# A planner that lets only one of ACT and DVE read a PSUM bank at a time

## The chip, the cores and the metric

One core of one Trainium2 chip runs the kernel. The metric is the device time of one execution in microseconds; 576.35 us is the median of three runs before the change (576.04 to 577.06).

## The reference

The kernel computes a trunk of two decoder layers on one sequence of 256 tokens, with 1024 features, in float32. Layer 0 mixes tokens by causal attention with 16 heads of 64 (with 256 tokens there is a single block of keys, so the choice of past blocks selects nothing). Layer 1 mixes them by attention with 12 heads in three groups, windows and dilations (128, 1), (512, 4) and (2048, 16), whose results are weighted by their softmax denominators. After each mixer stands a squared-ReLU MLP of width 4096. Cut to what matters:

```python
cos, sin = rotary_tables(S, x.dtype)
for i in range(2):
    mix = (moba_attention, dilated_attention)[i](h, w_qkv[i], w_o[i], cos, sin)
    h = layer_norm(ALPHA * h + mix, ln_mix_g[i], ln_mix_b[i])
    h = layer_norm(ALPHA * h + jnp.square(jax.nn.relu(h @ w_in[i])) @ w_out[i], ln_mlp_g[i], ln_mlp_b[i])

# in both mixers, before the scores
q = apply_rotary(qkv[:, :, 0], cos, sin) * (dh ** -0.5)
k = apply_rotary(qkv[:, :, 1], cos, sin)
# apply_rotary: [t1 * c - t2 * s, t2 * c + t1 * s]
```

## The kernel before

**The arithmetic.** Every float32 operand of a matmul is split in two parts of a narrower type, a high part (ACT copies it, line 316) and a low part (DVE subtracts, line 321), and each product is made of three matmuls: high by high, high by low, low by high. The weights arrive as tiles of 128x1024 (`raw`, four buffers, loads on SP, line 312) and become `whi` and `wlo`, ten buffers each. Matmuls are recorded on line 325, transposes on line 615.

**The banks.** PSUM has eight banks, tiles of 128x512 float32, under two tags of four each. `acc` holds the projections and the output sums; `tp` holds scores, transposes and the attention results.

**Attention.** A pair of heads goes through these steps: two weight tiles are projected into one `acc` bank (q in its left half, k in its right); `rotate` (line 530) turns that bank into the split, rotated q and k; the score matmuls fill `tp` banks; DVE adds the mask and takes the minimum (line 591); ACT takes the exponential (line 601); DVE scales (line 608); PE transposes into a `tp` bank; ACT copies that to `pt` (line 623); PE multiplies by v; and the result is split into `ahi` and `alo`. Layer 0 has 8 such pairs, layer 1 has 6. Two softmax-free stages follow in each layer: the output projection with its LayerNorm, and the MLP, whose weights make up most of the kernel's bytes.

**The rotation.** ACT copies the bank's lower 64 partitions to the upper half of a tile b and the upper to the lower (two instructions, line 544). DVE multiplies the bank by the first table into tile a (line 520), multiplies b by the second table in place, and adds b to a. Then ACT makes the high parts of q (line 316) and k (line 556), and DVE the low parts (lines 321 and 559, the latter through the helper of line 527). So three instructions read the bank: two of ACT and one of DVE. The copies and the multiply have no data in common but the bank.

**What sets the order.** Instructions aren't written in the order in which they run. Each is recorded as an operation with an engine, a cost in us and the buffers that it reads and writes. `Plan.order` (line 138) makes a first pass without contention for due times, and then simulates: for each engine it takes the operations that could start first (`start_of`, line 170: when the operands are there, the engine is free and a buffer of the tag is free), among these the one with the earliest due time, and of all engines the one that starts earliest; where two start at the same time ACT comes ahead of DVE. DVE may pass over a ready operation for a more urgent one that is about to be ready, if that saves over 0.2 us (`PATIENT`). Loads keep the order in which they were recorded. Costs are formulas, a copy of a half bank 512/1200 + 0.055 + 0.1 us, the multiply 512/960 + 0.07, and a result of ACT is there for DVE, or of DVE for ACT, after `LAT` = 0.14 us. The result is one list, sorted by simulated start, and it is emitted in that order; each engine then works through its share in order. The semaphores are set by the layer below, from the emitted order.

The dependences that the planner knows come from the buffers' readers and writers: a read after a write, a write after a read or a write. Two reads of one buffer are independent.

Of the kernel before, what the change touches and what calls it, by code (L numbers as in the profile page):

```python
# [54 lines left out]
def latency(p, q):  # L55
    if p.eng == "SP":
        return LANDED
    if p.eng == "PE":
        return 0.0 if q.eng == "PE" else PE_OUT
    return PE_IN if q.eng == "PE" else LATS.get((p.eng, q.eng), LAT)  # L60
# [3 lines left out]
def landed(t, bus, nbytes):  # L64
    t = max(t + FETCH, bus)
    return t + nbytes / RATES[t > BURST]


class Buf:


    def __init__(self, pool, shape, dtype, tag, name):
        self.pool, self.shape, self.dtype, self.tag, self.name = pool, shape, dtype, tag, name
        self.real = None
        self.state = {}
        self.left = 0
        self.held = False

    @property
    def t(self):  # L80
# [9 lines left out]
class Plan:  # L90
# [47 lines left out]
    def order(self):  # L138
        clock = {e: BEGIN[e] for e in ("PE", "SP")}
        bus = 0.0  # L140
        for o in self.ops:
            t = max([clock.get(o.eng, 0.0)] + [p.end + latency(p, o) for p in o.preds])
            o.end = t + o.cost
            if o.eng in clock:
                clock[o.eng] = o.end
            if o.xfer:
                bus = o.end = landed(t, bus, o.xfer)
            o.due = t - o.ahead if o.eng == "PE" else None
        t = clock["PE"]
        for o in reversed(self.ops):  # L150
            for q in o.succs:
                d = q.due - o.cost - latency(o, q)
                o.due = d if o.due is None else min(o.due, d)
            if o.due is None:
                o.due = t - o.early
        engines = sorted({o.eng for o in self.ops})
        free = {e: BEGIN[e] for e in engines}
        bus = 0.0
        cand = {e: [] for e in engines}
        slots = {tag: [0.0] * cap for tag, cap in self.caps.items()}  # L160
        done = []
        for o in self.ops:
            o.wait = len(o.preds)
            o.ready = 0.0
            if not o.wait:
                cand[o.eng].append(o)

        loads = [o for o in self.ops if o.eng == "SP"]

        def start_of(o):  # L170
            s = max(o.ready, free[o.eng])
            need = {}
            for b in o.bufs:
                if not b.held:
                    need.setdefault(b.tag, []).append(b)
            for tag, bs in need.items():
                q = self.queue[tag]
                spare = 0
                if {id(b) for b in q[: len(bs)]} != {id(b) for b in bs}:
                    if tag not in LOOSE:  # L180
                        return None
                    spare = 1
                if len(slots[tag]) < len(bs) + spare:
                    return None
                s = max(s, sorted(slots[tag])[len(bs) - 1])
            return s

        total = len(self.ops)
        while len(done) < total:
            best = None  # L190
            for e in engines:
                lst = [(start_of(o), o) for o in cand[e] if e != "SP" or o is loads[0]]
                lst = [x for x in lst if x[0] is not None]
                if not lst:
                    continue
                first = min(s for s, _ in lst)
                s, o = min((x for x in lst if x[0] <= first), key=lambda x: (x[1].due, x[1].n))
                if e in PATIENT:
                    worst = PATIENT[e]
                    now, ready = s, o  # L200
                    for s2, o2 in lst:
                        if now < s2 < now + ready.cost and o2.due < ready.due:
                            waits = max(s2 - o2.due, s2 + o2.cost - ready.due)
                            runs = max(now - ready.due, now + ready.cost - o2.due)
                            if runs - waits > worst:
                                worst, s, o = runs - waits, s2, o2
                if best is None or s < best[0]:
                    best = (s, o)
            assert best is not None
            s, o = best  # L210
            cand[o.eng].remove(o)
            if o.eng == "SP":
                loads.pop(0)
            for b in o.bufs:
                if not b.held:
                    slots[b.tag].remove(min(slots[b.tag]))
                    self.queue[b.tag].remove(b)
                    b.held = True
            cost = o.cost * 2 if o.eng == "PE" and s < PE_COLD else o.cost
            free[o.eng] = s + cost  # L220
            o.end = s + cost
            if o.xfer:
                bus = o.end = landed(s, bus, o.xfer)
            done.append((s, o.n, o))
            for b in o.bufs:
                b.left -= 1
                b.last = max(getattr(b, "last", 0.0), o.end + (PE_OUT if o.eng == "PE" else LAT))
                if not b.left:
                    slots[b.tag].append(b.last)
            for q in o.succs:  # L230
                q.wait -= 1
                q.ready = max(q.ready, o.end + latency(o, q))
                if not q.wait:
                    cand[q.eng].append(q)
        done.sort(key=lambda x: x[:2])
        return [o for _, _, o in done]
# [7 lines left out]


LOOSE = ("tp",)


LAYOUT = (
# [866 lines left out]
```

## Time and profile before

| what | value |
|---|---|
| median of three runs | 576.35 us |
| the profiled execution, its time | 576.27 us |
| the profiled execution, its span from the first to the last instruction | 574.5 us |
| mean granted TensorE clock | 0.997 |
| busy, PE (matmul) / PEld (weight load) | 561.4 / 486.1 us |
| busy, DVE / ACT / POOL | 418.9 / 313.8 / 8.4 us |
| instructions in the span | 8588 |
| moved by DMA | 105.61 MB, 184 GB/s on average |

Busy time of an engine is the time in which at least one of its instructions runs; weight loads overlap matmuls. In lists of instructions the first number is the start in us from the beginning of the span, the second the duration, then the engine, the line, the operation and the tiles (result<-operands); "x2" merges instructions that follow each other, and a bracket at the end gives how long the engine was idle before it and whose end it waited for. In lists of waits the columns are the total in us, the number of waits and the longest. Attention of layer 0 takes the span to about 110 us, its MLP lies between about 137 and 290, attention of layer 1 between about 312 and 375, and its MLP between about 403 and 566.

### The profile page before, as it was taken

What the parts mean: (1) busy time and instruction counts of PE and PEld (TensorE: products, weight loads), DVE (VectorE), ACT (ScalarE), POOL (GpSimd) and SP (SyncE); (2) the same over time, 40 slices, a digit from 0 to 9 for tenths busy, and PEclk for the clock granted to TensorE, in tenths of its full rate; (3) what the DMA queues carried; (4) which work ended last, traced back from release to release, by engine and by line L of the source; (5) the groups of instructions that cost most, each with busy time, mean ns of one, the idle gap of its engine ahead of it and who ended that gap; (6) DMA issues with size and microseconds to landing.
All of it is one profiled execution on the core that took longest, in us unless ns stands there. A gap on an engine that the chain in (4) does not pass through costs nothing.

```text
span 574.5 us, 8588 instructions
## 1 busy us (share of the span) xinstructions
PE 561.4 (98%) x3234; PEld 486.1 (85%) x3234; DVE 418.9 (73%) x729; ACT 313.8 (55%) x529; POOL 8.4 (1%) x13
## 2 busy tenths in 40 slices
PE   8999999999999999999999999999999999999994
PEld 7898898788888888888888997878888888888884
DVE  5898879798775675675678698878966756756644
ACT  6887878456554554455533586844754544544400
POOL 0000000010000000000000000000000000000000
PEclk9999999999999999999999999999999999999998
DMA  8676753627877565555526534534888655655101
GB/s 323 222 242 210 245 184 111 193 83 242 266 274 241 186 212 185 186 189 182 189 80 176 215 129 136 177 111 139 266 261 252 210 187 177 194 186 181 37 1 73
DMA packets 30282, 105.61 MB, mean 184 GB/s; under 512 B 3489, under 2 KB 4257, under 8 KB 30241
## 3 DMA queue, kind: packets, MB, share of 16 engines
q1 hardware_dynamic: 30240, 105.07, 55.8%
q8 instruction: 25, 0.41, 0.3%
q14 instruction: 17, 0.13, 0.1%
HBM read 104.01 MB, written 1.05 MB: 183 GB/s over the span
## 4 chain that ended last, share of the span: by engine, by line
PE 87%; DMA 4%; ACT 4%; DVE 3%; issue 1%; SPq 0%; DVEq 0%; ACTq 0%
PE acc L325 49%; PE tp L325 36%; DMA raw<-in_wv_dram 2%; PE tp L615 2%; ACT whi L316 1%; DVE wlo L321 1%; ACT ta L544 1%; DVE ta L520 1%; DMA raw<-in_wqk_dram 1%; DMA raw<-in_xw_dram 1%; ACT sc L601 0%; DVE tok L527 0%; DVE klo L527 0%; ACT pt L623 0%; ACT khi L556 0%
## 5 line engine op out<-in xcount | busy, mean ns | idle before, releaser
L321 DVE TENSOR_TENSOR wlo<-raw,whi 128x1024 fp32r<-128x1024 f32 (+2 forms) x185 | 222.0, 1206 | 91.4 <-ACT whi L316 91.0
L316 ACT ACTIVATE whi<-raw 128x1024 fp32r<-128x1024 f32 (+2 forms) x184 | 191.0, 1047 | 147.8 <-PE tp L325 69.9
L325 PE MATMUL acc<-whi,ahi 128*128 128x512 f32 (+1 forms) x312 | 119.5, 383 | 0.0
L325 PE MATMUL acc<-wlo,ahi 128*128 128x512 f32 (+1 forms) x312 | 117.3, 380 | 0.0
L325 PE MATMUL tp<-xs,whi 128*128 128x512 f32 x448 | 112.0, 392 | 0.0
L325 PE MATMUL acc<-whi,alo 128*128 128x512 f32 (+1 forms) x312 | 100.7, 379 | 0.0
L325 PEld LDWEIGHTS tp<-xs,whi 128*128 128x128 f32 x448 | 81.1, 189 | 14.9
L325 PEld LDWEIGHTS acc<-whi,ahi 128*128 128x128 f32 x312 | 58.7, 188 | 11.3 <-issue 0.9
L325 PEld LDWEIGHTS acc<-wlo,ahi 128*128 128x128 f32 x312 | 58.7, 188 | 10.4
L325 PE MATMUL acc<-xs,whi 128*128 128x256 f32 x448 | 65.1, 287 | 0.9 <-ACT xs L316 0.6
L325 PEld LDWEIGHTS acc<-whi,alo 128*128 128x128 f32 x312 | 57.1, 188 | 10.5
L325 PEld LDWEIGHTS tp<-xs,wlo 128*128 128x128 f32 x448 | 61.0, 190 | 4.2
L325 PE MATMUL tp<-xs,wlo 128*128 128x256 f32 x448 | 62.6, 283 | 0.0
L325 PEld LDWEIGHTS acc<-xs,whi 128*128 128x128 f32 x448 | 58.6, 192 | 3.0 <-ACT xs L316 1.1
L316 ACT ACTIVATE ahi<-ta 128x256 fp32r<-128x256 f32 x56 | 22.8, 407 | 27.6 <-DVE ta L527 27.5
L325 PE MATMUL acc<-xs,wlo 128*128 128x256 f32 x224 | 36.5, 284 | 0.0
L325 PEld LDWEIGHTS acc<-xs,wlo 128*128 128x128 f32 x224 | 31.0, 192 | 0.7 <-issue 0.7
L325 PE MATMUL acc<-whi,xs 128*128 128x512 f32 (+1 forms) x112 | 28.2, 362 | 0.0
L321 DVE TENSOR_TENSOR alo<-ta,ahi 128x256 fp32r<-128x256 f32 x56 | 23.4, 421 | 6.2 <-ACT ahi L316 6.2
L520 DVE TENSOR_TENSOR ta<-tp,ta 128x256 f32<-128x256 f32 x56 | 23.5, 420 | 5.8 <-ACT ta L769 5.8
L769 ACT ACTIVATE ta<-tp 128x256 f32<-128x256 f32 x56 | 21.0, 375 | 9.3 <-PE tp L325 9.3
L544 ACT ACTIVATE ta<-acc 64x512 f32<-64x512 f32 x28 | 16.6, 593 | 17.4 <-DVE ta L520 11.2
(85 smaller groups left out, 531.8 us busy)
## 6 DMA issues: line engine op xcount, KB each, us to landing
raw<-in_win_dram SPq DMA_DIRECT2D x64, 512.0 KB, 4.3
raw<-in_wout_dram SPq DMA_DIRECT2D x64, 512.0 KB, 4.2
raw<-in_wqk_dram SPq DMA_DIRECT2D x24, 512.0 KB, 4.3
raw<-in_wo_dram SPq DMA_DIRECT2D x14, 512.0 KB, 3.4
raw<-in_wv_dram SPq DMA_DIRECT2D x8, 512.0 KB, 6.7
g<-in_lng_dram SPq DMA_DIRECT2D x4, 512.0 KB, 5.8
b<-in_lnb_dram SPq DMA_DIRECT2D x4, 512.0 KB, 7.8
raw<-in_wv1a_dram SPq DMA_DIRECT2D x4, 512.0 KB, 3.3
```

What stands on the lines that cost most here:

```text
L316: op("ACT", act(n, sbuf=sbuf), lambda: nc.scalar.activation(hi(), src(), AF.Copy), r, whi)
L321: lambda: nc.vector.tensor_tensor(lo(), src(), f32(hi()), op=ALU.subtract), list(r) + list(whi), wlo,
L325: nc.tensor.matmul(out_ap, lhsT, rhs, start=start, stop=stop)
L520: op("DVE", dve(n) + extra, lambda: nc.vector.tensor_tensor(out_ap(), a(), b(), op=alu), r, w)
L544: lambda h=h: nc.scalar.activation(b.t[64 * h : 64 * h + 64, :], ps.t[64 - 64 * h : 128 - 64 * h, :], AF.Copy),
L615: nc.tensor.transpose(ps.t[:, c : c + P], src(), ident.t)
L769: op("ACT", act(S), lambda: nc.scalar.activation(u(), ps.t[:, S:], AF.Copy), [ps], uk)
```

## The change

Each buffer remembers the last operation outside PE that was placed on it. When the planner asks when an operation of ACT or DVE could start, and this operation uses a buffer of one of the PSUM tags whose last such operation was another engine's, the start is no earlier than that operation's end plus the latency between the two engines (0.14 us between ACT and DVE). The first pass, the due times, the costs and the instructions themselves stay as they are; only the order in which they are emitted can differ. The whole diff:

```diff
@@ class Buf
         self.left = 0
         self.held = False
+        self.reader = None
@@ Plan.order, start_of
             for b in o.bufs:
                 if not b.held:
                     need.setdefault(b.tag, []).append(b)
+                elif b.tag in BANKS and o.eng != "PE" and b.reader and b.reader.eng != o.eng:
+                    s = max(s, b.reader.end + latency(b.reader, o))
@@ Plan.order, after an operation is placed
             for b in o.bufs:
+                if o.eng != "PE":
+                    b.reader = o
                 b.left -= 1
@@
 LOOSE = ("tp",)
+
+BANKS = ("tp", "acc")
```

## The prediction

> **What bounds the kernel now.** I read the page first, then the busy times by stretch, then the waits, then the timelines of the engines around each wait. The page says who is full and which group carries the instructions that the change is about:
>
> ```profile
> PE 561.4 (98%) x3234; PEld 486.1 (85%) x3234; DVE 418.9 (73%) x729; ACT 313.8 (55%) x529; POOL 8.4 (1%) x13
> PE 87%; DMA 4%; ACT 4%; DVE 3%; issue 1%; SPq 0%; DVEq 0%; ACTq 0%
> L544 ACT ACTIVATE ta<-acc 64x512 f32<-64x512 f32 x28 | 16.6, 593 | 17.4 <-DVE ta L520 11.2
> ```
>
> PE is busy 561.4 of 574.5 us and makes up 87% of the chain. So only 13.1 us of the span are PE idle time, and a new order that leaves the matmuls as they are can win only there, apart from hidden gaps, which I come to. By stretch (the columns are the stretch, its length, then busy us and instructions of PE, PEld, DVE, ACT and POOL, then clock, DMA share and GB/s):
>
> ```profile
> 0.00:10.00 10.00, 7.93 (x42) 6.71 (x43) 5.42 (x15) 6.47 (x12) 0.76 (x5) 1.00 0.82 291
> 40.00:50.00 10.00, 9.04 (x71) 7.88 (x69) 8.60 (x21) 8.77 (x20) 0.00 (x0) 1.00 0.80 270
> 137.00:290.00 153.00, 153.00 (x776) 130.60 (x776) 102.35 (x144) 77.43 (x113) 0.00 (x0) 1.00 0.65 212
> 324.00:345.00 21.00, 21.00 (x168) 20.56 (x167) 20.25 (x52) 16.82 (x31) 0.00 (x0) 1.00 0.43 144
> 345.00:365.00 20.00, 18.60 (x151) 16.59 (x150) 17.30 (x45) 14.21 (x25) 0.00 (x0) 1.00 0.38 114
> 545.00:575.00 30.00, 22.06 (x120) 19.02 (x118) 13.39 (x27) 0.80 (x2) 1.84 (x2) 0.94 0.10 36
> ```
>
> The reader is to see three things. The start leaves 2.07 us idle and the end 7.94 (its 30 us hold 0.5 beyond the span, so 7.4 are real); neither holds a rotation, so the change can't touch them. The long MLP stretch is full to the last tenth. What the change can reach lies in the attention stages: 0.96 us at 40 to 50, 1.40 at 345 to 365 and some tenths elsewhere. The waits name the cause:
>
> ```profile
> ACT ta L544 <- DVE ta L520: 11.2, 12, 2.7
> DVE ta L520 <- ACT ta L544: 11.8, 14, 3.6
> PEld tp L615 <- ACT pt L623: 3.5, 3, 1.5
> PE tp L615 <- ACT pt L623: 2.6, 3, 1.3
> PE tp L615 <- DVE mx L591: 0.3, 1, 0.3
> ```
>
> The first row is the point of the case. Line 544 copies halves of the projected bank into tile b, line 520 multiplies the same bank into tile a. Neither reads what the other writes, yet ACT waits 12 times for DVE. The two are kept apart in the bank they both read, in the order in which the planner emits them; and the planner, which knows only data dependences, believes that they overlap. Three PE waits for a pt copy and one for a mask make up 2.9 us, and the timelines show that the rotation stands ahead of each:
>
> ```profile
> 18.43 1.20 ACT L544 ACTIVATE ta<-acc 64x512 f32<-64x512 f32 x2
> 44.10 0.59 ACT L544 ACTIVATE ta<-acc 64x512 f32<-64x512 f32 x1
> 45.46 0.59 ACT L544 ACTIVATE ta<-acc 64x512 f32<-64x512 f32 x1 [0.76 <-DVE ta L520]
> 46.07 1.06 ACT L316 ACTIVATE whi<-raw 128x1024 fp32r<-128x1024 f32 x1
> 47.04 0.58 ACT L623 ACTIVATE pt<-tp 128x512 f32<-128x512 f32 x1
> 92.06 0.59 ACT L544 ACTIVATE ta<-acc 64x512 f32<-64x512 f32 x1 [0.76 <-DVE ta L520]
> 93.19 0.57 ACT L623 ACTIVATE pt<-tp 128x512 f32<-128x512 f32 x1
> 347.13 0.59 ACT L544 ACTIVATE ta<-acc 64x512 f32<-64x512 f32 x1 [0.76 <-DVE ta L520]
> 347.75 1.09 ACT L623 ACTIVATE pt<-tp 128x512 f32<-128x512 f32 x2
> ```
>
> ```profile
> 47.67 0.44 PE L615 MATMUL tp<-ident,sc 128*128 128x128 f32 x2 [0.96 <-ACT pt L623]
> 61.24 0.84 PE L615 MATMUL tp<-ident,sc 128*128 128x128 f32 x6 [0.31 <-DVE mx L591]
> 93.82 0.44 PE L615 MATMUL tp<-ident,sc 128*128 128x128 f32 x2 [0.33 <-ACT pt L623]
> 348.40 0.65 PE L615 MATMUL tp<-ident,sc 128*128 128x128 f32 x4 [1.33 <-ACT pt L623]
> ```
>
> Read the first block from 44.10: first half copy, 0.76 us of nothing while DVE multiplies, second half copy, a weight split, then the pt copy, which frees the tp bank that PE waits for at 47.67. The same string ends at 93.82 and at 348.40.
>
> **The change part by part.** It adds and removes no instruction, byte or matmul. The planner gains one wait: an ACT or DVE operation on a tp or acc bank whose last reader was the other engine starts no sooner than that reader's end plus a latency.
>
> *Where it bites.* For a split or a squared ReLU the second reader already waits by data for the first, with the same latency, so nothing moves. Masks are DVE alone, pt and v copies ACT alone. That leaves the 14 rotations (28 copies in the group's row). In five of them the multiply already stands before or behind both copies; the 18.43 row is such a pair. In nine it stands between, nine of the 12 waits above.
>
> *What the planner does instead.* Once the first copy is placed, the multiply may start only at its end plus 0.14 us, while the second copy may start at the end itself; it is the earlier candidate and is taken first. So I expect the nine to become copy, copy, multiply. If DVE is free first, the multiply leads and ACT is given other work. What one such change gives is in these rows:
>
> ```profile
> 19.66 0.69 DVE L520 TENSOR_TENSOR ta<-acc,ropet 128x512 f32<-128x512 f32 x1
> 20.27 0.68 DVE L520 TENSOR_TENSOR ta<-ta,ropet 128x512 f32<-128x512 f32 x1
> 46.08 0.69 DVE L520 TENSOR_TENSOR ta<-ta,ropet 128x512 f32<-128x512 f32 x1 [0.32 <-ACT ta L544]
> 54.24 0.69 DVE L520 TENSOR_TENSOR ta<-acc,ropet 128x512 f32<-128x512 f32 x1 [0.82 <-ACT ta L544]
> 55.59 0.69 DVE L520 TENSOR_TENSOR ta<-ta,ropet 128x512 f32<-128x512 f32 x1 [0.66 <-ACT ta L544]
> 60.32 0.42 DVE L591 CUSTOM_DVE_ANT_0 sc<-tp,m 128x256 f32<-128x256 f32 x1
> ```
>
> On ACT, the second copy ends 1.20 us after the first began instead of 45.46 + 0.59 − 44.10 = 1.95: 0.75 sooner, the idle 0.76. On DVE, the grouped pattern reaches the second multiply at 20.27 − 18.43 = 1.84 us after the first copy's start. The interleaved one takes 46.08 − 44.10 = 1.98. So the rotated q and k come 0.14 us sooner, not later, although the first multiply starts later. That answers what stands behind the new wait: the multiply holds only the table product behind it, which must wait for the second copy anyway, and DVE may run a mask or a weight split in the time.
>
> *What PE gets.* At 47.67 the pt copy comes 0.76 sooner; the gap is 0.96, so 0.76 goes and 0.20 stays. At 93.82 the gap is 0.33 and all goes. At 348.40 0.76 of 1.33 goes and 0.57 stays; there what is late next is still the pt copy, behind the rotation. At 61.24 PE waits for the masks that DVE ran from 60.32, behind the rotation of 54.24; I take the 0.14 us of the shorter DVE string, between 0 (a split slips in) and the gap's 0.31 (the masks move into DVE's idle 0.82 and 0.66). Sum: 0.76 + 0.33 + 0.76 + 0.14 = 1.99 us.
>
> The five interleaved rotations that are left I cost at nothing: PE runs projection matmuls beside them (21.00 of 21 us at 324 to 345). From 137 on the MLP is full, so what is won before it stays won; its order depends on the same due times, which the edit doesn't touch. SP's loads follow a fixed list and start when raw buffers come free; ACT's earlier splits free these up to 0.76 us sooner, and at a DMA share of 0.80 and less a load that starts earlier lands earlier or as before. POOL computes only the LayerNorm powers and no queue of it is passed. The acc bank is given back after 1.23 + 0.69 = 1.92 us instead of 1.95, the same.
>
> *A price that before doesn't show* is what the new clock does to all other choices of the planner. The nearest rows bound it: below, no more than the gaps at the four places can go; above, a split placed ahead of a multiply costs DVE about 1.2 us (below). I take it as nothing, because the row of 324 to 345 is nearest to it: three rotations beside a DVE busy 96% of the time, and PE still lost nothing there. Both ends stay for the range.
>
> The profiled execution took 576.27 us with its span of 574.5; the median of the three runs is 576.35. The sum on the execution gives a span of 572.5 and 574.28; on the median, 576.35 − 1.99 = 574.36. I say **574.4**.
>
> A hint that the page understates PE's room: the Trainium skill (Perfetto Trace Analysis, Identifying the Most-Contended Engine) judges TensorE's headroom by weight-load time and not by matmul time. By the PEld row the three pt waits are 3.5 us and not 2.6, so the gap at 93.82 would give up to 0.76 and the sum would be up to 2.4; the rows here do differ that way.
>
> **The rivals.**
>
> *More: the four gaps close wholly.* While DVE waits for two copies instead of one, it can run the masks, which free the score banks, so that the transposes no longer depend on the pt copy. For it: DVE's idle 0.82 and 0.66 around 54.24. The most this gives is the PEld gaps, 3.5, and the one at 61.21:
>
> ```profile
> 61.21 0.64 PEld L615 LDWEIGHTS tp<-ident,sc 128*128 128x128 f32 x6 [0.71 <-issue]
> ```
>
> 3.5 + 0.7 = 4.2 us, 572.2. Against: pt copies are ACT's, and the masks there come due later than the rotation.
>
> *About nothing: the saved ACT time goes to something else.* The string to the pt copy holds a weight split of 1.06 (46.07), and a planner that sees 0.76 us free on ACT may put another ahead of the pt copy. At two of the three places that takes the gain back; 0.33 + 0.14 = 0.47 would stay: 575.9. For it: splits of 1.06 wait at ACT all through these stages. Against: pt copies have PE behind them and come due early.
>
> *The change doesn't do what it says*, the emitted order being as before: 576.35. The 12 waits of ACT for DVE speak against it.
>
> *Slower: a split gets in front of the multiply.* Now that the multiply must wait for both copies, the planner can fill DVE's time with a weight split that is still running when the second copy ends. Place: layer 1, where the scores follow the last part of q by little:
>
> ```profile
> 337.00 0.42 DVE L321 TENSOR_TENSOR qlo<-ta,qhi 128x256 fp32r<-128x256 f32 x1
> 337.33 1.23 DVE L321 TENSOR_TENSOR wlo<-raw,whi 128x1024 fp32r<-128x1024 f32 x1
> 362.53 0.42 DVE L321 TENSOR_TENSOR qlo<-ta,qhi 128x256 fp32r<-128x256 f32 x1
> ```
>
> ```profile
> 337.53 0.33 PE L325 MATMUL tp<-khi,qlo 128*128 128x256 f32 x1
> 363.00 0.39 PE L325 MATMUL tp<-khi,qlo 128*128 128x256 f32 x1
> ```
>
> The margins are 337.53 − 337.42 = 0.11 us and 363.00 − 362.95 = 0.05, and DVE is busy 20.25 of 21 us at 324 to 345. A split of 1.23 in front makes q late by up to 1.23 − 0.14 = 1.09. It decides when three scores are hit with no projection left for PE: 3 × 1.09 − 1.99 = +1.28, 577.6. Against: the planner knows the wait now, lets DVE hold out for an urgent operation when that saves over 0.2 us, and can give PE the next projection.
>
> **How the numbers follow.** Forecast 0.45, more 0.11, nothing gained 0.17, no effect 0.05, slower 0.22. A measurement of this kernel can tell about 0.2%, 1.15 us, from no change: below 575.2 is faster, above 577.5 slower. The first two cases are faster, 0.56; the next two within, 0.22; the last slower, 0.22. The forecast's own range is 573.5 to 575.2. The range runs from 572.2, all gaps gone, to 577.6, the slower rival at its point of decision, which leaves out about half of that rival.
>
> **What would show it.** Right: ACT's copies stand in pairs of 1.20; the row of ACT waiting for DVE falls from 11.2 us in 12 to under 4; the three pt waits of PE fall from 2.6 to under 1; 137 to 290 stays full, only earlier by about 1.2. Wrong: the pairs are there but PE has new gaps before scores (a wait for DVE qlo or klo) or before transposes; or PE's instructions around 40 to 110 and 318 to 365 run in another order with as much idle time; or the MLP stretch itself has new gaps.

## The result, and the profile after

The changed kernel takes 572.49 us (median of six runs, 572.26 to 573.19), the kernel before 576.21 beside it. The ratio is 0.9934, 95% interval 0.9921 to 0.9947: 3.7 us faster, by the interval 3.1 to 4.6. Its profiled execution has a span of 570.8 us.

The first lines of the page of the changed kernel, and its stretches (columns as before):

```profile
PE 560.9 (98%) x3234; PEld 487.0 (85%) x3234; DVE 418.6 (73%) x729; ACT 314.4 (55%) x529; POOL 8.4 (1%) x13
PE 97%; DMA 1%; DVE 1%; ACT 0%; issue 0%; SPq 0%; DVEq 0%
```

```profile
0.00:10.00 10.00, 8.12 (x37) 6.98 (x38) 4.89 (x14) 6.04 (x12) 0.76 (x5) 1.00 0.80 286
40.00:50.00 10.00, 10.00 (x82) 9.41 (x82) 9.15 (x21) 8.36 (x21) 0.00 (x0) 1.00 0.86 294
137.00:290.00 153.00, 153.00 (x776) 130.63 (x775) 101.23 (x143) 75.65 (x111) 0.00 (x0) 1.00 0.66 212
345.00:365.00 20.00, 20.00 (x154) 17.94 (x153) 18.49 (x48) 15.96 (x32) 0.00 (x0) 1.00 0.45 150
```

The work is the same, PE's busy time too (560.9 and 561.4), but PE's share of the chain has risen from 87% to 97%: the chain hardly leaves PE any more. The stretches at 40 to 50 and 345 to 365, where 0.96 and 1.40 us were idle, are full. The whole list of PE's waits in the changed kernel shows why:

```profile
PE tp L332 <- DVE warm L417: 1.2, 1, 1.2
PE tp L332 <- ACT xs L323: 0.6, 2, 0.3
PE acc L332 <- ACT xs L323: 0.4, 1, 0.4
PE acc L332 <- DVE xs L328: 0.3, 1, 0.3
```

No pt copy and no mask is among them: all four gaps are gone entirely. What is left is the start and the LayerNorms. To see where the time went, I take four points on PE that every version has: the first score, the first transpose of the first LayerNorm's output, that of the second's, and the end of the span. Before, and then after:

```profile
28.16 0.39 PE L325 MATMUL tp<-khi,qhi 128*128 128x512 f32 x1
118.00 0.27 PE L615 MATMUL tp<-ident,tok 128*128 128x128 f32 x1
297.39 0.82 PE L615 MATMUL tp<-ident,tok 128*128 128x128 f32 x6
```

```profile
28.74 0.39 PE L332 MATMUL tp<-khi,qhi 128*128 128x512 f32 x1
116.06 1.03 PE L622 MATMUL tp<-ident,tok 128*128 128x128 f32 x8
295.47 1.03 PE L622 MATMUL tp<-ident,tok 128*128 128x128 f32 x8
```

The differences of these starts are the stages: attention of layer 0 with its output projection from 89.84 to 87.32 us, 2.52 less; its MLP 179.39 and 179.41, the same; the rest, which holds layer 1, up to the ends of the spans, from 277.11 to 275.33, 1.78 less. The changed kernel's first score stands 0.58 later: its first loads landed later (ACT waits 1.99 us for the third of them, before 1.39), and a later start partly comes back as a shorter first gap (e6 shows that, below), so up to 0.58 of the 2.52 may be the start's. What is sure goes by the time from the span's start: the first LayerNorm's transposes begin 1.94 us earlier (116.06 for 118.00), and the rest takes 1.78 less. Together 3.72 us, the same as the medians.

Inside a rotation the order isn't the one that I forecast:

```profile
ACT ta L551 <- DVE ta L527: 12.2, 7, 4.8
DVE ta L527 <- ACT ta L551: 2.7, 5, 1.3
```

ACT still waits for DVE, for as long as before (11.2), only less often. In all 14 rotations the emitted order is multiply, copy, copy. PE before, just ahead of the first gap:

```profile
43.40 0.40 PE L325 MATMUL tp<-khi,qhi 128*128 128x512 f32 x1
44.45 0.60 PE L615 MATMUL tp<-ident,sc 128*128 128x128 f32 x4
```

The stretch that answers to it, on ACT, DVE and PE of the changed kernel (not every row):

```profile
44.61 0.60 ACT L630 ACTIVATE pt<-tp 128x512 f32<-128x512 f32 x1 [1.28 <-PE tp L622]
46.05 0.37 ACT L630 ACTIVATE pt<-tp 128x256 f32<-128x256 f32 x1
46.45 1.20 ACT L551 ACTIVATE ta<-acc 64x512 f32<-64x512 f32 x2
```

```profile
44.38 0.69 DVE L527 TENSOR_TENSOR ta<-acc,ropet 128x512 f32<-128x512 f32 x1
45.30 0.42 DVE L598 CUSTOM_DVE_ANT_0 sc<-tp,m 128x256 f32<-128x256 f32 x1 [0.24 <-PE tp L332]
```

```profile
43.97 0.60 PE L622 MATMUL tp<-ident,sc 128*128 128x128 f32 x4
44.33 0.48 PE L332 MATMUL tp<-khi,qhi 128*128 128x512 f32 x1
45.45 0.38 PE L622 MATMUL tp<-ident,sc 128*128 128x128 f32 x2
```

Before, PE issued the scores first, then four transposes, and then stood still at the last two until a pt copy that came behind both copies of the rotation and a weight split. Now the four transposes come ahead of the scores, the pt copies ahead of the rotation's copies, and the masks in one go while ACT is at work elsewhere. The rotation's copies start 2.35 us later than before (46.45 and 44.10), and no wait of PE comes of it. That isn't a rotation with a wait less; it is another plan.

### The profile page after: what moved, and what is told of

Its sections match the earlier page's. It is cut to its first block, busy times and chain, and to the rows that moved or that the text cites. A ratio compares the mean times of both kernels' runs of the same rounds, so it can differ in the third digit from the quotient of the medians.

```text
span 570.8 us, 8590 instructions
## 1 busy us (share of the span) xinstructions
PE 560.9 (98%) x3234; PEld 487.0 (85%) x3234; DVE 418.6 (73%) x729; ACT 314.4 (55%) x529; POOL 8.4 (1%) x13
## 4 chain that ended last, share of the span: by engine, by line
PE 97%; DMA 1%; DVE 1%; ACT 0%; issue 0%; SPq 0%; DVEq 0%
PE acc L332 56%; PE tp L332 39%; PE tp L622 3%; DMA raw<-in_xw_dram 1%; DVE tok L534 0%; ACT ta L786 0%; ACT xs L323 0%; SPq L319 0%; ACT whi L323 0%; DVE bst L717 0%; DVE xs L328 0%; DVEq L1117 0%; DVE wlo L328 0%; DVE mv L720 0%; DVE rstd L721 0%
## 5 line engine op out<-in xcount | busy, mean ns | idle before, releaser
L332 PE MATMUL tp<-whi,xs 128*128 128x512 f32 x80 | 24.7, 396 | 0.6 <-ACT xs L323 0.6
```

Source lines behind the costliest of these rows:

```text
L332: nc.tensor.matmul(out_ap, lhsT, rhs, start=start, stop=stop)
```

## The experiments

These theories were set against each other, the third of them after the first four runs.

- **Local**: the lost time was ACT's 0.76 us inside a rotation; any order without the multiply between the copies gives the gain. This was the prediction's sum.
- **Replanning**: the gain lies in the new plan around the rotation; the plan keeps it whatever the order inside the rotation is.
- **Agreement**: the gain comes because the planner's clock now agrees with the chip, so that the lists of PE, ACT and DVE fit each other; the order within a rotation matters little, so long as the planner knows it.
- **Chance**: the planner's choices are so sensitive that any reshuffle may win or lose such an amount.

Twelve kernels ran, each 5 to 11 times, beside the kernel before. The stages are those of above, from one profile each, which may be up to 0.75 us off the kernel's median (e7's is of an execution of 574.24 us, e8's of 572.65); "start" is the time up to the first score.

| run | median us | before | ratio (95%) | start | attention 0 | MLP 0 | rest |
|---|---|---|---|---|---|---|---|
| before | | | 1 | 28.16 | 89.84 | 179.39 | 277.11 |
| changed | 572.49 | 576.21 | 0.9934 (0.9921–0.9947) | 28.74 | 87.32 | 179.41 | 275.33 |
| e1_mul_first | 577.44 | 576.40 | 1.0023 (1.0014–1.0032) | 28.49 | 89.54 | 179.41 | 277.66 |
| e2_copies_first | 576.84 | 576.40 | 1.0008 (0.9999–1.0017) | 28.79 | 89.52 | 179.41 | 277.38 |
| e4_copies_first_four | 575.75 | 576.40 | 0.9987 (0.9978–0.9995) | 29.39 | 89.27 | 179.41 | 276.43 |
| e3_after_interleaved | 576.71 | 576.40 | 1.0004 (0.9995–1.0013) | 28.46 | 91.21 | 179.41 | 275.82 |
| e5_layer0_only | 574.41 | 576.20 | 0.9968 (0.9955–0.9980) | 28.79 | 87.30 | 179.42 | 277.09 |
| e6_layer1_only | 574.58 | 576.20 | 0.9971 (0.9959–0.9982) | 28.93 | 89.30 | 179.42 | 275.45 |
| e7_copies_alloc_first | 573.49 | 576.20 | 0.9954 (0.9941–0.9968) | 28.27 | 88.52 | 179.42 | 276.19 |
| e8_interleaved_known | 573.31 | 576.20 | 0.9948 (0.9935–0.9960) | 28.75 | 87.36 | 179.45 | 275.24 |
| c1_lat12_norule | 576.47 | 576.52 | 0.9997 (0.9988–1.0006) | 28.41 | 89.31 | 179.41 | 277.17 |
| c2_lat16_norule | 576.58 | 576.52 | 0.9999 (0.9990–1.0007) | 28.61 | 89.30 | 179.40 | 277.59 |
| a1_lat12_rule | 572.89 | 576.52 | 0.9942 (0.9928–0.9955) | 28.52 | 87.70 | 179.42 | 275.46 |
| a2_lat16_rule | 573.86 | 576.52 | 0.9946 (0.9933–0.9958) | 29.49 | 87.95 | 179.44 | 275.22 |

### The local edits: before's plan with another order in the rotation

Each rotation records its two copies `b0`, `b1` and its multiply `a`, and the finished list is edited before it is emitted; all else stays.

```diff
         ops = self.order()
+        for b0, b1, a in self.rots:
+            if ops.index(b0) < ops.index(a) < ops.index(b1):
+                ops.remove(a)
+                ops.insert(ops.index(b0), a)        # e1; in e2: ops.insert(ops.index(b1) + 1, a)
```

> Before's order, unchanged but for one thing: in the nine rotations that have the multiply between the two copies, the multiply is moved directly ahead of the first copy. Local theory (a wait inside the rotation is all that was lost): this is the order that the changed kernel has in all 14 rotations, so it should give most of its 3.7 us, 572.5 to 573.5. Replanning theory (the gain comes from what the planner puts beside the rotation and into PE's order, now that it knows the real ends): ACT still spends 0.73 us waiting for the multiply and 1.20 on the copies, together 1.93 against 1.95, so next to nothing is won: 575.7 to 576.5, and PE's gaps before the transposes stay near 2.6 us.

> Before's order, but in the nine rotations the multiply is moved directly behind the second copy: the order that the prediction expected of the planner. The prediction's sum holds for this kernel to the letter: pt copies 0.76 us sooner, PE's gaps lose 0.76 + 0.33 + 0.76 + 0.14 = 1.99 us, 574.2, and about 0.8 us of waits for pt copies stay. Local theory in its strong form (the whole gain of the change lies in the rotation): 572.5. If the replanning is all: 576.2.

Both miss the local theory. With the multiply in front (e1), which is the order of the changed kernel and stands here in 13 of the 14 rotations, the kernel is 0.2% slower, which the replanning theory didn't expect either (575.7 to 576.5). ACT waits 18.3 us in 12 waits for the multiply in e1, and 11.2 before. With the copies in front (e2), the very kernel that my sum describes, it is not faster by 2 us but the same. The rows of e2 show where the gain went. PE at the places of the four gaps, then ACT at the third, then DVE at the first:

```profile
48.43 0.65 PE L330 MATMUL tp<-pt,v 128*64 128x256 f32 x4 [0.49 <-DVE mx L597]
61.24 0.85 PE L621 MATMUL tp<-ident,sc 128*128 128x128 f32 x6 [0.16 <-DVE mx L597]
94.13 0.44 PE L621 MATMUL tp<-ident,sc 128*128 128x128 f32 x2 [0.66 <-ACT pt L629]
348.28 0.66 PE L621 MATMUL tp<-ident,sc 128*128 128x128 f32 x4 [0.49 <-ACT pt L629]
```

```profile
90.70 1.20 ACT L549 ACTIVATE ta<-acc 64x512 f32<-64x512 f32 x2 [0.39 <-PE acc L330]
92.99 0.51 ACT L607 ACTIVATE sc<-sc,mx 128x256 f32<-128x256 f32 x1 [1.10 <-DVE mx L597]
93.50 0.58 ACT L629 ACTIVATE pt<-tp 128x512 f32<-128x512 f32 x1
```

```profile
45.67 0.69 DVE L525 TENSOR_TENSOR ta<-acc,ropet 128x512 f32<-128x512 f32 x1 [0.74 <-ACT ta L549]
46.28 0.41 DVE L597 CUSTOM_DVE_ANT_0 sc<-tp,m 128x256 f32<-128x256 f32 x1
46.62 0.69 DVE L525 TENSOR_TENSOR ta<-ta,ropet 128x512 f32<-128x512 f32 x1
```

The last gap shrinks from 1.33 to 0.49, the one at 61.24 from 0.31 to 0.16, as forecast (0.76 and 0.14). The first is no longer a wait for the pt copy, but PE now waits 0.49 for a mask, which stands on DVE behind the multiply that has been moved back. At 94.13 the gap has doubled, from 0.33 to 0.66: ACT has its copies done early, but the next thing in its list is an exponential, which waits 1.10 us for that same kind of mask, and the pt copy stands behind it. The time taken from ACT was put on DVE: before, DVE ran a mask while it waited for the second copy, and that mask, still next in DVE's list, now starts only after the late multiply. With the first copy at 44.45, the second multiply starts 46.62 − 44.45 = 2.17 us later, and not 1.84 as I had reckoned, nor 1.98 as before. Even so the four gaps are 1.13 us smaller in all (1.80 for 2.93); the rest of the answer is in the next run.

> As the run with the copies first, but only in the four rotations that stand ahead of PE's four gaps; the other five keep the multiply between the copies. The prediction costs those five at nothing, so this run should take the time of the run with all nine, within 0.3 us. If the five matter it is slower than that run by up to 0.76 us for each.

With only the four rotations ahead of the gaps, the kernel is 0.13% faster, 575.75, and that is 1.1 us faster than with all nine. Those are the five rotations that I had costed at nothing. By the table they cost 0.95 us in the rest (277.38 against 276.43); the 0.25 in layer 0 (89.52 against 89.27) is no more than plans of this kind scatter there. The weight loads of e2 show what it is:

```profile
337.92 0.19 PEld L330 LDWEIGHTS tp<-klo,qhi 128*128 128x128 f32 x1 [0.21 <-DVE klo L532]
363.02 0.19 PEld L330 LDWEIGHTS tp<-khi,qhi 128*128 128x128 f32 x1 [0.48 <-ACT qhi L321]
```

With a third of 0.15 (338.26, for qlo) these are 0.84 us of waits for parts of q and k ahead of scores, which neither the kernel before nor e4 has. They stand at the two places for which the prediction's slower rival had reckoned margins of 0.11 and 0.05 us. So these expectations miss too, and no edit of this kind reaches the changed kernel.

### The reverse: the changed plan with the old order in the rotation

```diff
         ops = self.order()                          # of the changed planner
+        for b0, b1, a in self.rots:
+            ops.remove(a)
+            ops.insert(ops.index(b0) + 1, a)
```

> The changed kernel's order, but in all 14 rotations the multiply is put back between the two copies. Local theory: the gain goes, 575.5 to 576.5. Replanning theory: PE's order and the place of the pt copies and masks stay as the changed planner set them, and only ACT's 0.76 us of idle time comes back where ACT has room: most of the gain stays, 572.5 to 574.

576.71: the gain goes, as the local theory said, but the stages say something else. Attention of layer 0 takes 91.21 us, 1.4 more than in the kernel before, while the rest keeps most of its gain (275.82). PE has three gaps before transposes there. The first is the one at 61.24 of the kernel before, now 0.99 us for 0.31; the other two stand where neither kernel had any:

```profile
61.80 0.85 PE L627 MATMUL tp<-ident,sc 128*128 128x128 f32 x6 [0.99 <-DVE mx L603]
85.02 0.44 PE L627 MATMUL tp<-ident,sc 128*128 128x128 f32 x2 [0.62 <-ACT pt L635]
100.74 0.66 PE L627 MATMUL tp<-ident,sc 128*128 128x128 f32 x4 [0.53 <-ACT pt L635]
```

My expectation for the replanning theory (572.5 to 574) missed as well: in layer 0 the new plan alone is worth nothing, if the rotation isn't what the plan takes it for. In the rest it does keep 1.29 of its 1.78 us, so there the misfit costs little. What layer 0 says, that plan and rotation must agree, is the agreement theory, and the runs that follow were set for it.

### The old order, known to the planner

Tile b is asked for ahead of tile a, and the second copy may not be placed before the multiply; the rule for the banks stays. So every rotation is copy, multiply, copy, and the planner knows what that costs.

```diff
+                if b.rot and o is b.rot[1] and b.rot[2] not in placed:
+                    return None
...
-        a = mk([P, 512], F32, "ta", 4)
         b = mk([P, 512], F32, "ta", 4)
+        a = mk([P, 512], F32, "ta", 4)
```

> The changed planner, but every rotation is forced to copy, multiply, copy, the order that cost ACT 0.76 us of idle time in the kernel before, and now the planner knows that wait. Agreement theory: most of the gain is there all the same, 572.5 to 574, because masks and pt copies are placed where they are really ready. Local theory (the interleaved order is the loss): as before or slower, 576 to 577.

573.31, ratio 0.9948 (0.9935 to 0.9960), which overlaps with that of the changed kernel; the stages are 87.36 and 275.24, the same as its 87.32 and 275.33. The order in the rotation is the bad one, that of nine rotations before, and the gain is there. ACT at the first rotation that had cost PE a gap:

```profile
46.34 0.59 ACT L556 ACTIVATE ta<-acc 64x512 f32<-64x512 f32 x1
46.84 0.50 ACT L614 ACTIVATE sc<-sc,mx 128x256 f32<-128x256 f32 x1
47.33 0.50 ACT L614 ACTIVATE sc<-sc,mx 128x256 f32<-128x256 f32 x1
47.95 0.59 ACT L556 ACTIVATE ta<-acc 64x512 f32<-64x512 f32 x1
```

The planner has put two exponentials between the copies, and the time in which ACT would wait for the multiply is used: in the whole kernel ACT waits 3.0 us in 3 waits for it, and 11.2 in 12 before.

> The changed planner, and in each rotation tile b is asked for ahead of tile a, so that the copies may go first: the planner then really chooses copy, copy, multiply in 12 of 14 rotations, and knows what it costs. Agreement theory: the order inside the rotation matters little so long as the planner knows it, 572 to 573.5. Forecast's theory (two copies in a row free ACT 0.76 us sooner, and the rotated parts come 0.14 sooner than in any other order): faster than the changed kernel, 571.5 to 572.3. If the multiply in front is what made the gain: 575 to 576.5.

With b asked for first and no more, the planner chooses copy, copy, multiply in 12 of 14 rotations: 573.49, also most of the gain, and not more than the changed kernel, as the forecast would have it. Its layer 0 (88.52) keeps one gap of 0.89 us for a pt copy:

```profile
46.39 0.39 PE L332 MATMUL tp<-khi,qhi 128*128 128x256 f32 x1 [0.89 <-ACT pt L630]
```

So three orders inside the rotation, each known to the planner, give 0.9934, 0.9948 and 0.9954, and the same orders unknown to it give 1.0004 to 1.0023.

The planner's own simulation, which the kernels' code contains, fits this. It puts the first score at 28.41 and the first LayerNorm's transposes at 112.37 us in the kernel before and in the changed one alike, and the last operation's end at 562.51 and 563.27. So to the planner the rule is no gain at all, rather a small loss. What the rule changes is how much of the plan the chip can keep: those transposes start at 118.00 and 116.06.

### One layer at a time

```diff
-                elif b.tag in BANKS and o.eng != "PE" and b.reader and b.reader.eng != o.eng:
+                elif b.guard and o.eng != "PE" and b.reader and b.reader.eng != o.eng:
...
+        ps.guard = ropet is ropes[0]                # e5: layer 0; e6: is not
```

> The changed planner, but the rule holds only for the eight rotations of layer 0. Agreement theory (the gain comes where the planner's clock agrees with the chip, stage by stage): attention of layer 0 falls from 89.8 to 87.3 us and the rest stays as before, 573.9 in all. If the layers need each other, or if the gain of layer 0 is chance, it is another value: 576.4 for none.

> The changed planner, but the rule holds only for the six rotations of layer 1. Agreement theory: attention of layer 0 stays at 89.8 us, layer 1's attention and what follows give the other 1.4 and 0.4 us, 574.6 in all. With the kernel for layer 0 alone the two gains should add up to 3.7 to 4.3 us. If they don't, the gain isn't made stage by stage.

574.41 and 574.58, gains of 0.32% and 0.29%, which add up to 0.61% against 0.66%. In us that is 3.4, a little under the 3.7 to 4.3 expected, and the first run is 0.5 over its 573.9; the intervals cover both. The rule looks here at no bank but the rotations', so nothing else that it covers is needed for the gain. The stages fall where they should: 87.30 for the ruled layer 0 with 277.09 left as it was, and 275.45 for the ruled layer 1. In the second run layer 0 has before's plan, and yet takes 89.30 for 89.84. Its first score stands at 28.93 for 28.16, and the last two transposes of the first gap, which waited 0.96 before, wait less:

```profile
47.93 0.44 PE L624 MATMUL tp<-ident,sc 128*128 128x128 f32 x2 [0.46 <-ACT pt L632]
```

0.50 of the later start comes back there. So one profile settles this stage to half a microsecond, as the other plans without the rule show too (89.27 to 89.84); those with it, left as planned, lie from 87.30 to 88.52. The gain is made stage by stage.

### Reshuffles with and without the rule

```diff
-LAT = 0.14
+LAT = 0.12                                          # c1, a1; in c2, a2: 0.16
```

> The kernel before, with no rule for the banks, and only the planner's latency between engines set from 0.14 to 0.12 us: a reshuffle that tells the planner nothing of the banks. Agreement theory: the rotations still cost what the planner doesn't know, 575.3 to 577.5. Chance theory (any other order is as likely as the changed one to win 3 to 4 us): it may land anywhere, 572 to 580.

> As the run before it, with the latency at 0.16 us: another reshuffle without the rule. Agreement theory: 575.3 to 577.5. Chance theory: 572 to 580.

> The changed kernel with the latency at 0.12 us: a reshuffle that keeps the rule. Agreement theory: 572 to 574, since the planner still knows the wait. Chance theory: it falls back towards 576 or beyond as often as not.

> The changed kernel with the latency at 0.16 us: a second reshuffle that keeps the rule. Agreement theory: 572 to 574, and perhaps a little under the changed kernel. Chance theory: towards 576 or beyond.

All four came out as the agreement theory had it: 576.47 and 576.58 without the rule, ratios 0.9997 and 0.9999, and 572.89 and 573.86 with it, 0.9942 and 0.9946. The longest waits of PE of the second reshuffle without the rule, and all of the first with it:

```profile
PE tp L615 <- ACT pt L623: 2.1, 3, 1.3
PE tp L325 <- ACT xs L316: 1.2, 3, 0.6
PE tp L325 <- DVE warm L410: 1.2, 1, 1.2
PE tp L615 <- DVE mx L591: 0.3, 1, 0.3
```

```profile
PE tp L332 <- DVE warm L417: 1.2, 1, 1.2
PE acc L332 <- ACT xs L323: 0.7, 1, 0.7
PE tp L332 <- ACT xs L323: 0.6, 2, 0.3
PE acc L332 <- DVE xs L328: 0.3, 1, 0.3
```

Without the rule the pt copies and the mask hold PE up again, 2.4 us; with it none does. Chance moves these plans by some tenths of a microsecond to one; it didn't move one by 3.7. The two sides aren't equally strong. The reshuffles without the rule are small: 14 and 13 of the 14 rotations keep their order, and, counted engine by engine in the lists that the kernels' code gives, 19 and 33 of 3259 operations have to be moved to get from before's list to theirs, against 147 for the changed kernel's. With the rule 81 and 115 have to be moved from the changed kernel's list, and the gain stays. A plan as far from before's as the changed one, made without the rule, wasn't run. No run beats the changed kernel beyond its interval, so there is no better version to show.

## Why the prediction was right, and where it wasn't

**The direction and the place were right.** PE is the bound, the room is its idle time, and that lay behind rotations whose bank ACT and DVE both read. "Where it bites" held: e5 and e6 apply the rule to the rotations' banks alone. The MLP stayed as it was (179.39 and 179.41). The gain was forecast as 1.99 us and measured as 3.7. The interval, 572.2 to 577.6, holds 572.49 near its lower end; the forecast's own range, 573.5 to 575.2, doesn't.

**"What the planner does instead" failed.** I expected copy, copy, multiply; the planner emits multiply, copy, copy. I had looked at starts and latencies, and overlooked the buffers: tiles of the tag `ta` are given out in the order in which they were asked for, and a is asked for ahead of b. A copy can't be placed until the multiply has its tile. Before the change it then went back in simulated time to start beside the multiply; under the rule it can't. e7 shows it: with b asked for first, the copies lead in 12 rotations. With that step the sign "ACT's wait falls under 4 us" fell too (12.2), while the signs of the closed pt gaps and the full MLP came.

**"What PE gets" failed, and that its sign came out right is luck.** The sum moved the pt copies forward by ACT's 0.76 and held all else still. e2 is that sum as a kernel, and it gains nothing (1.0008). Two of its four terms were right (0.84 measured for 0.76 at the last gap, 0.15 for 0.14 at the mask). The other two came to 0.47 for 0.76 and to a loss of 0.33 for a gain of 0.33, by masks that the later multiply had pushed behind it. The step "0.14 us sooner" was read from a rotation with no mask between its multiplies; with one, the second multiply starts 0.19 later than before (2.17 for 1.98). And the five rotations "at nothing" cost 1.1 us in e2, so the 1.13 won at the gaps is gone. The whole gain came through the term that the prediction did name and took as nothing, "what the new clock does to all other choices of the planner". What the runs put in the sum's place: a wait that the planner doesn't know delays one engine against a plan made for three, and each of them works its list in order. Moving one instruction moves the misfit; a plan made with the wait removes it. e3 and e8 are the pair that shows this: the same order in the rotation, 576.71 with a plan that doesn't know it and 573.31 with one that does.

**The rivals.** The one called "more" came about in size and in part in mechanism: all four gaps closed, by its estimate 4.2 us, measured 3.7; and the masks did move into DVE's waiting time (45.30), and the pt copies moved ahead as well. I gave it 0.11 because I held the rest of the plan still. The hint from the Trainium skill (Perfetto Trace Analysis, Identifying the Most-Contended Engine) came nearer here: by weight loads PE's waits at the gaps were 4.2 us, by matmuls 2.9, and 3.7 came back (the interval from 3.1 takes in the one and not the other). The slower rival didn't come about in the changed kernel: no wait for a part of q or k stands in the list of PE's waits above. In e2, without a new plan, its effect did, 0.84 us at the places that it named, though by masks and not by a weight split.

**What stays open.** How much of layer 0's 2.52 us is the later start's. The first score lies between 28.16 and 29.49 in the 14 profiles whatever the rule, so I take that for the loads' scatter, and no run held it fixed. Against e6, c1 and c2 (89.30, 89.31, 89.30), whose first scores stand within 0.33 us of the changed kernel's, the stage is 2.0 us shorter, the same as the 1.94 above. Why e7 keeps a gap of 0.89 us in a plan that knows the wait is open too, and so is how a far reshuffle without the rule would do.

## What to carry to other kernels

A planner that emits the instruction order should know every wait that the layer below it will add, shared banks among them; here that was worth 0.66%, and it showed as waits between engines that exchange no data. When such a wait is found, don't judge its price by the idle time beside it, and don't mend the finished list by hand: give the planner the wait and let it plan anew. Before trusting the gain, reshuffle the plan with and without the rule, and see how far each reshuffle really goes.

## What the runs showed of the hardware

One number is useful: the hand-over of a bank between ACT and DVE took 0.04 us here. In the kernel before, the first copy of the rotation at 44.10 ends at 44.69, the multiply starts at 44.73 and ends at 45.42, and the second copy starts at 45.46:

```profile
44.73 0.69 DVE L520 TENSOR_TENSOR ta<-acc,ropet 128x512 f32<-128x512 f32 x1 [0.18 <-ACT ta L544]
```

That is 0.04 us each way, where the planner reckons with 0.14. In eight of the nine interleaved rotations of the kernel before ACT's idle time is the same 0.76 us. So the price of a bank that two engines read was here the time of the other's read, 0.69 us, and hardly the hand-over.
